# Attention scored a head at a time, and a planner that may move casts and two-tensor operations between engines

## The chip, the cores and the metric

The kernel runs on one core of a Trainium2 chip. The metric is device time in microseconds (us), from several runs of the same program. One execution of it was recorded by the hardware profiler; every row below comes from that one.

## The reference, cut to what matters

A trunk of two layers works on 512 tokens of width 1024. Each layer is a norm, one input projection, three token mixers that read the same normalised input (A windowed attention, B gated DeltaNet, C RWKV-7), an output projection with residual, and a gated MLP with a width-3 convolution.

```python
def banded_window_attention(q, k, v, sink):        # 6 heads, 2 kv heads, 4 query blocks of 128
    s = jnp.einsum('bnqhgd,bnkhd->bnhgqk', qb, kw) * (HEAD_DIM ** -0.5)
    s = jnp.where(valid, s, -jnp.inf)               # +-128 tokens: 2 or 3 key blocks a query block
    m = jnp.maximum(jnp.max(s, -1, keepdims=True), sk)
    p = jnp.exp(s - m)
    p = p / (jnp.sum(p, -1, keepdims=True) + jnp.exp(sk - m))
    o = jnp.einsum('bnhgqk,bnkhd->bnqhgd', p, vw)
...
for l in range(DEPTH):                              # 2
    h = rms_norm(x, norm_mix[l])
    proj = h @ w_in[l]
    mixed = concatenate([attention, deltanet, rwkv](proj))
    x = x + mixed @ w_out[l]
    h = rms_norm(x, norm_ffn[l])
    x = x + conv_ffn(h, ffn_w_up[l], ffn_conv[l], ffn_w_down[l])
return rms_norm(x, norm_final)
```

DeltaNet and RWKV are computed in chunks of 64 tokens, and both need the inverse of many small triangular blocks.

## The kernel before

**Layout and products.** Activations lie as 128 channels by 512 tokens. Every large product is made of pieces of which each operand is split in a high and a low part (type fp32r): activations in `hh`/`hl` (function `split`), weights in `wh`/`wl` (function `weights`). A weight tile comes as `wr` by DMA, 128 x 512 for four blocks of 128 x 128; `wh` is a cast of it (`S.activation(hi, raw, AF.Copy)`, ScalarE, ACT), and `wl` is `wr` minus `wh` (GpSimd, POOL). Function `product` then issues three matmuls a block: `wh` by `hh`, `wh` by `hl`, `wl` by `hh`. There are 408 weight tiles, and three buffers each for `wr`, `wh`, `wl`.

**Stages of a layer**, with times of layer 0: input projections, token shifts (`token_shift`), RWKV preparation (`rwkv_prep`) and the first inversion (`invert`) to about 195 us; the rest of that inversion (`finish_inverse`) and RWKV's scan to about 297; DeltaNet's inversion (`invert_both`) from 297 to 351, and its `finish_inverse` to 373; DeltaNet's scan (`dn_scan`) to 412; gates, output projection (`w_out`) and norm to 468; the MLP's up-projection to 730 and its down-projection to 840. The up-projection goes through 22 pairs a layer of 48 matmuls each: a gate tile (`tr`) and a value tile (`td`). After each pair VectorE (DVE) scales both from PSUM (`TENSOR_TENSOR td<-ps,rb`), makes the convolution's outer taps with four `SCALAR_TENSOR_TENSOR`, multiplies the two and subtracts the high part; ScalarE or VectorE makes the middle taps (`td<-tr,fixed`, `tr<-td,fixed`), and ScalarE the silu and the high part (`p<-tr`).

**invert_both** (lines 837 to 858) is a chain on VectorE of 30 steps: a product into `cv` (`cv<-pair_sq`) and a sum back into `pair_sq` (`pair_sq<-pair_sq,cv`), each step reading what the last wrote. Between, four transposes before and after.

**Attention.** `attn_head` (line 1299) handles one pair of query heads. For each of four query blocks it makes two score matmuls and two fused mask-and-maximum operations on VectorE (`CUSTOM_DVE_ANT_0 cv<-ps,fixed`, maximum in `mx`), then on 128 x 2 numbers the sink's difference (`es`), the negated maximum (`nmx`), the exponential of `es`; two exponentials with sum (`cv<-cv,nmx`, the sum in `den`); `den` plus `es`, its reciprocal; two normalisations (`cv<-cv,den`), transposes on TensorE, a copy to `tr`, and the product with the values. It yields after each block. Three heads a layer; `layer` calls `next(att, None)` five times among the 31 steps of `invert_both` and once after every step of `dn_scan`, and what is left after it.

**What sets the order.** Nothing above is issued as written. `V`, `S`, `G`, `PE` and `SY` are recorders: class `Plan` notes each operation, its reads and writes, and a cost (`price`). `schedule` is a list scheduler over five engines: it places the ready operation with the smallest `prio`, which is minus the longest path of costs behind it minus the number that table `LEAD` gives to the operation's task. 37 names stand in the table, the same number for both layers. It holds an operation back while the tile that it writes has no room, and prices TensorE (PE) at twice the cost after a long idle time (`COLD`) until enough work has been placed (`WARM`). A VectorE operation of two tensors that starts while POOL is busy is priced longer (`contend`). An operation with an alternative (`other`) goes to whichever of two engines is free first: here copies and scalings of float32 may move between ScalarE and VectorE, but none that writes fp32r, and no operation of two tensors. The trace names line 516, where `call` is made, for nearly every instruction; so rows are told apart by operation and tile.

## Time and profile before

| | before |
|---|---|
| three runs, us | 1677.74, 1678.78, 1680.12 |
| the profiled execution, us | 1681.65 |
| its span, us | 1679.5 |
| TensorE busy | 1531.1 us, 91%, 11500 matmuls |
| VectorE | 1083.1 us, 64% |
| ScalarE | 736.2 us, 44% |
| GpSimd | 645.2 us, 38% |
| DMA | 126.07 MB |

The span is the time from the first to the last recorded instruction; about 2 us of the profiled execution lie outside it. A share of busy time is an average over stages. The windows below tell them apart: for each stretch, its length, then busy time and count for PE, PEld (weight loads), DVE, ACT, POOL, then the TensorE clock that was granted as a share of 2.4 GHz.

### The profile page before, as it was taken

What the parts mean: (1) busy time and instruction counts of PE and PEld (TensorE: products, weight loads), DVE (VectorE), ACT (ScalarE), POOL (GpSimd) and SP (SyncE); (2) the same over time, 40 slices, a digit from 0 to 9 for tenths busy, and PEclk for the clock granted to TensorE, in tenths of its full rate; (3) what the DMA queues carried; (4) which work ended last, traced back from release to release, by engine and by line L of the source; (5) the groups of instructions that cost most, each with busy time, mean ns of one, the idle gap of its engine ahead of it and who ended that gap; (6) DMA issues with size and microseconds to landing.
All of it is one profiled execution on the core that took longest, in us unless ns stands there. A gap on an engine that the chain in (4) does not pass through costs nothing. (4 is left out here: it accounts for less than half of the span.)

```text
span 1679.5 us, 29012 instructions
## 1 busy us (share of the span) xinstructions
PE 1531.1 (91%) x11500; PEld 1192.8 (71%) x11500; DVE 1083.1 (64%) x1689; ACT 736.2 (44%) x1399; POOL 645.2 (38%) x510
## 2 busy tenths in 40 slices
PE   7999787589999999999999996966899999999996
PEld 5677665367777777788876775644677877777885
DVE  7799977967437666740058998789654566766101
ACT  5565345454543433332236544355544433334221
POOL 5422332010555554555552232410017454555553
PEclk9999889779999999999999997996799999999998
DMA  6312303010233333333342121120003333333332
GB/s 177 84 34 76 70 20 89 13 34 2 71 91 100 94 89 95 94 106 112 108 105 64 47 75 39 54 86 1 27 14 89 94 88 95 95 93 88 115 91 85
DMA packets 230536, 126.07 MB, mean 75 GB/s; under 512 B 23656, under 2 KB 221416, under 8 KB 230400
## 3 DMA queue, kind: packets, MB, share of 16 engines
q1 hardware_dynamic: 228624, 121.02, 25.8%
q10 hardware_dynamic: 1776, 3.20, 0.7%
q8 instruction: 90, 1.47, 0.3%
q14 instruction: 46, 0.38, 0.1%
HBM read 117.84 MB, written 6.34 MB: 74 GB/s over the span
## 5 line engine op out<-in xcount | busy, mean ns | idle before, releaser
L516 POOL TENSOR_TENSOR wl<-wr,wh 128x512 fp32r<-128x512 f32 (+1 forms) x408 | 558.1, 1379 | 830.1 <-ACT wh L516 667.9
L516 PE MATMUL ps<-hh,wh 128*128 128x512 f32 x1248 | 457.6, 399 | 6.9 <-ACT wh L516 6.9
L516 ACT ACTIVATE wh<-wr 128x512 fp32r<-128x512 f32 (+1 forms) x408 | 243.5, 616 | 495.9 <-PE ps L516 433.9
L516 PE MATMUL ps<-hh,wl 128*128 128x512 f32 x1248 | 452.9, 398 | 7.4 <-POOL wl L516 5.3
L516 PE MATMUL ps<-hl,wh 128*128 128x512 f32 x1248 | 451.6, 394 | 0.0
L516 PEld LDWEIGHTS ps<-hh,wl 128*128 128x128 f32 x1248 | 232.7, 187 | 84.2 <-POOL wl L516 30.3
L516 PEld LDWEIGHTS ps<-hh,wh 128*128 128x128 f32 x1248 | 233.6, 188 | 69.8 <-ACT wh L516 16.2
L516 PEld LDWEIGHTS ps<-hl,wh 128*128 128x128 f32 x1248 | 233.8, 188 | 51.7 <-issue 3.4
L516 DVE TENSOR_TENSOR p<-ps,p 128x512 f32<-128x512 f32 (+2 forms) x72 | 38.2, 551 | 197.4 <-PE ps L516 197.1
L516 PE MATMUL ps<-p,wh 128*128 128x512 f32 x512 | 158.2, 389 | 0.0
L516 DVE TENSOR_TENSOR td<-ps,rb 128x512 f32<-128x512 f32 (+1 forms) x64 | 43.7, 688 | 136.4 <-PE ps L516 136.3
L516 PEld LDWEIGHTS ps<-p,wh 128*128 128x128 f32 x512 | 96.1, 188 | 19.9
L516 DVE SCALAR_TENSOR_TENSOR tr<-td,fixed,tr 128x511 f32<-128x511 f32 x88 | 105.3, 1197 | 0.6 <-ACT tr L516 0.4
L516 PE MATMUL ps<-p,wl 128*128 128x512 f32 x256 | 99.8, 390 | 0.0
L516 ACT ACTIVATE p<-p 32x256 f32<-32x256 f32 (+3 forms) x112 | 66.0, 589 | 16.1 <-DVE p L516 11.2
L516 PE MATMUL ps<-fixed,cv 128*128 128x128 f32 x168 | 36.6, 338 | 38.8 <-ACT cv L516 35.7
L516 DVE SCALAR_TENSOR_TENSOR td<-tr,fixed,td 128x511 f32<-128x511 f32 x88 | 70.8, 805 | 0.3
L516 PE MATMUL ps<-p,p 32*32 32x32 f32 (+2 forms) x1232 | 56.1, 253 | 14.9 <-DVE p L516 11.3
L516 DVE TENSOR_TENSOR tr<-tr,td 128x512 f32<-128x512 f32 x44 | 67.3, 1529 | 1.6
L516 ACT ACTIVATE p<-ps 64x256 f32<-64x256 f32 (+4 forms) x113 | 44.9, 401 | 52.7 <-PE ps L516 33.3
L516 PEld LDWEIGHTS ps<-sm,p 64*64 64x64 f32 x1344 | 49.4, 145 | 24.6 <-DVE sm L516 12.9
L516 PEld LDWEIGHTS ps<-p,p 32*32 32x32 f32 (+1 forms) x1232 | 51.3, 143 | 21.5 <-DVE p L516 12.1
(170 smaller groups left out, 2089.5 us busy)
## 6 DMA issues: line engine op xcount, KB each, us to landing
wr<-ffn_w_up SPq DMA_DIRECT2D x176, 256.0 KB, 2.8
wr<-w_in SPq DMA_DIRECT2D x88, 256.0 KB, 2.8
wr<-ffn_w_down SPq DMA_DIRECT2D x80, 256.0 KB, 2.9
p<-scr ACTq DMA_DIRECT2D x12, 256.0 KB, 5.1
wr<-w_in SPq DMA_DIRECT2D x24, 128.0 KB, 2.6
wr<-w_out SPq DMA_DIRECT2D x32, 96.0 KB, 2.6
wr<-w_out SPq DMA_DIRECT2D x16, 192.0 KB, 2.6
p<-xt SPq DMA_DIRECT2D x8, 256.0 KB, 4.5
```

The costliest lines, as they stand in the source:

```text
L516: tc.keep_in_program_order(call(*args, **kw))
```

## The change

Four things are changed.

1. `attn_head` handles a head as a whole. All eight score matmuls and mask-and-maximum operations come first and keep their scores in eight `cv` tiles; `es`, `nmx` and the exponential of `es` are made once on 128 x 8 numbers, then come eight exponentials, one `den` plus `es`, one reciprocal, and after these the four blocks' normalisations, transposes and products. It yields seven times a head, each phase a group of its own for `LEAD`.
2. `other` gives more operations an alternative: casts that write fp32r (`wh`, `hh`, the high parts `p`, `cv`, `at` of the MLP's gates) may go to VectorE, and a `tensor_tensor` of SBUF tiles with 128 or more columns may move between VectorE and GpSimd.
3. `LEAD` has a number for each task of each layer (letters `a` and `b`), each phase of `attn_head` and each `token_shift`, some 120 in all.
4. `schedule` prices TensorE's clock by equal stretches (`BEAT`) of the planned time: one with too little weighted work in it (`DOWN`, `WEIGHT`) makes matmuls cost twice later on, until one with enough (`UP`) has passed. An operation that was GpSimd's and goes to VectorE is now priced longer beside a busy GpSimd too. `wake` looks again at what blocks a held operation. `hh` and `hl` ask for one buffer instead of two, which `tile` overrides as before (64).

```diff
 LEAD = {
-    "attn_head0": -17500, "attn_head1": 13500, "attn_head2": 4300, "attn_proj": 281000, "dn_gates": 100400, "dn_out0": 5100,
...
+    "attn_head0a.0": -125700, "attn_head0a.1": 35000, "attn_head0a.3": -50200, "attn_head0a.4": 1596100, "attn_head0a.5": 341900, "attn_head0a.6": -258200,
...
     def other(self, o, name, reads, writes):
-        if not self.flexible or not writes or len(reads) < 1 or "float32r" in str(writes[0].dtype) or reads[0].dtype != F32:
+        if not writes or not reads:
             return None
...
-        if o.eng == "DVE" and name == "tensor_copy":
+        if o.eng == "DVE" and name == "tensor_copy" and src.dtype == F32:
...
+        if name == "tensor_tensor" and not psum and n >= 128 and len(dst.shape) == 2 and o.eng in ("DVE", "POOL"):
+            e, f, cost = ("POOL", self.nc.gpsimd, 180 + 2.3 * n) if o.eng == "DVE" else ("DVE", self.nc.vector, 165 + 1.04 * n)
+            return e, f.tensor_tensor, o.args, o.kw, cost
...
-                if t - free[e] > self.COLD:
-                    cold, heat = True, 0.0
-                if cold:
+                while t >= edge:
+                    slow = here < (self.UP if slow else self.DOWN) * self.BEAT
+                    here, then, edge = then, 0.0, edge + self.BEAT
+                if slow:
                     cost *= 2
...
-            elif o.contend and e == "DVE" and free["POOL"] > t:
+            elif e == "DVE" and (o.contend or o.eng == "POOL") and free["POOL"] > t:
                 cost += min(cost, free["POOL"] - t)
...
     def attn_head(l, tq, q, k, vt, dst):
-        po = ps("r")
-        for nb in range(4):
...
+        scs = [[cv() for g in range(2)] for nb in range(4)]
+        mxt, nmx, es, den = (tiny(8, tag=tag) for tag in ("mx", "nmx", "es", "den"))
+        for nb, (k0, k1) in enumerate(span):
...
+                PE.matmul(pss[:, :W], q[hs, P * nb : P * nb + P], k[hs, P * k0 : P * k0 + W], start=True, stop=True)
+                V.tensor_tensor_reduce(scs[nb][g][:, :W], ...
+        yield
+        V.tensor_tensor(by(es), sinkb[l][:, tq : 6 : 3].unsqueeze(1).broadcast_to([P, 4, 2]), by(mxt), sub)
+        V.tensor_scalar(nmx, mxt, -1.0, None, mult)
+        S.activation(es, es, AF.Exp)
+        for nb, (k0, k1) in enumerate(span):
...
+                S.activation(scs[nb][g][:, :W], scs[nb][g][:, :W], AF.Exp, bias=nmx[:, u], accum_out=den[:, u])
+        yield
+        V.tensor_tensor(den, den, es, add)
+        V.reciprocal(den, den)
+        po = ps("r")
+        for nb, (k0, k1) in enumerate(span):
...
+                V.tensor_scalar(scs[nb][g][:, :W], scs[nb][g][:, :W], den[:, u], None, mult)
...
```

How instructions stand now is told by both orders. First, VectorE inside `invert_both` of layer 0: `pair_sq` and `cv_563` are the chain's tiles, `mx`, `es` and `den` attention's. Before, one query block's operations lie between the steps at a time:

```order
L516 TENSOR_TENSOR pair_sq<-pair_sq,cv_563 128x2x14x17
L516 TENSOR_TENSOR cv_563<-pair_sq 128x468
L516 ISA cv_589,mx_591<-ps_592,fixed 128x384
L516 ISA mx_591 128x1
L516 TENSOR_TENSOR pair_sq<-pair_sq,cv_563 128x2x13x18
L516 TENSOR_TENSOR cv_563<-pair_sq 128x456
L516 ISA cv_590,mx_591<-ps_593,fixed 128x384
L516 ISA mx_591 128x1
L516 TENSOR_TENSOR es_595<-fixed,mx_591 128x2
L516 TENSOR_TENSOR pair_sq<-pair_sq,cv_563 128x2x12x19
```

Now, in the same chain:

```order
L546 CAST wh_816<-wr_815 128x512
L546 TENSOR_TENSOR cv_563<-pair_sq 128x260
L546 TENSOR_TENSOR pair_sq<-pair_sq,cv_563 128x2x26x5
L546 TENSOR_TENSOR cv_563<-pair_sq 128x300
L546 TENSOR_TENSOR pair_sq<-pair_sq,cv_563 128x2x25x6
L546 TENSOR_TENSOR den_575<-den_575,es_574 128x8
L546 RECIPROCAL den_575<-den_575 128x8
L546 TENSOR_TENSOR cv_563<-pair_sq 128x336
L546 TENSOR_SCALAR cv_569<-cv_569,den_575 128x384
L546 TENSOR_SCALAR cv_571<-cv_571,den_575 128x256
L546 TENSOR_SCALAR cv_565<-cv_565,den_575 128x256
L546 TENSOR_SCALAR cv_567<-cv_567,den_575 128x384
```

The whole head's `den` stands near the chain's start, four normalisations and a weight cast stand on VectorE between its steps, and after them the chain runs long stretches without a row of attention.

Second, VectorE in the up-projection of layer 0, the work of one pair. Before:

```order
L516 TENSOR_TENSOR td_1142<-ps_1135,rb_848 128x512
L516 TENSOR_TENSOR tr_1132<-ps_1125,rb_848 128x512
L516 TENSOR_SCALAR td_1133<-tr_1132,fixed 128x512
L516 SCALAR_TENSOR_TENSOR tr_1143<-td_1142,fixed,tr_1143 128x511
L516 SCALAR_TENSOR_TENSOR td_1133<-tr_1132,fixed,td_1133 128x511
L516 SCALAR_TENSOR_TENSOR tr_1143<-td_1142,fixed,tr_1143 128x511
L516 SCALAR_TENSOR_TENSOR td_1133<-tr_1132,fixed,td_1133 128x511
L516 TENSOR_TENSOR tr_1124<-tr_1124,td_1133 128x512
L516 TENSOR_TENSOR p_1134<-tr_1124,p_1134 128x512
```

Now:

```order
L546 CAST wh_1113<-wr_1112 128x512
L546 CAST wh_1120<-wr_1119 128x512
L546 TENSOR_TENSOR td_1106<-ps_1099,rb_812 128x512
L546 TENSOR_SCALAR tr_1107<-td_1106,fixed 128x512
L546 SCALAR_TENSOR_TENSOR tr_1107<-td_1106,fixed,tr_1107 128x511 x2
L546 CAST wh_1129<-wr_1128 128x512
L546 TENSOR_TENSOR tr_1096<-ps_1089,rb_812 128x512
L546 TENSOR_SCALAR td_1097<-tr_1096,fixed 128x512
L546 SCALAR_TENSOR_TENSOR td_1097<-tr_1096,fixed,td_1097 128x511 x2
L546 TENSOR_TENSOR tr_1088<-tr_1088,td_1097 128x512
L546 CAST p_1098<-tr_1088 128x512
L546 TENSOR_TENSOR p_1098<-tr_1088,p_1098 128x512
```

In this pair three weight casts and the cast of the gate's high part have come to VectorE, some of them ahead of or between the four taps.

Third, TensorE at the end of `dn_scan` of layer 0: `ps<-p,sm` is the scan, `ps<-hh,wh` and its like are the output projection, `ps<-td,fixed` a sum of `dn_out`. Before:

```order
L516 MATMUL ps_795<-p_541,sm_776 64x64 x2
L516 MATMUL ps_815<-p_541,sm_797 64x64 x2
L516 MATMUL ps_818<-p_541,sm_817 64x64 x2
L516 MATMUL ps_850<-hh_832,wl_853 128x512
L516 MATMUL ps_861<-hh_832,wl_864 128x512
L516 MATMUL ps_820<-td_819,fixed 128x512
L516 MATMUL ps_850<-hh_834,wh_852 128x512
```

Now (`at` holds queries, keys and values, `tr` the transposed probabilities):

```order
L546 MATMUL ps_745<-p_541,sm_744 64x64 x2
L546 MATMUL ps_764<-at_436,at_508 128x256
L546 MATMUL ps_765<-at_436,at_508 128x256
L546 MATMUL ps_784<-td_783,fixed 128x512
L546 MATMUL ps_696<-tr_711,at_456 64x128
L546 MATMUL ps_696<-tr_724,at_456 64x128 x3
L546 MATMUL ps_696<-tr_737,at_456 64x128 x2
L546 MATMUL ps_696<-tr_713,at_456 64x128
L546 MATMUL ps_696<-tr_726,at_456 64x128 x3
L546 MATMUL ps_696<-tr_739,at_456 64x128 x2
L546 MATMUL ps_787<-td_786,fixed 128x512
L546 MATMUL ps_814<-hh_792,wh_816 128x512
```

The last head's scores, the second head's products with the values and, further on, the last head's transposes and products now follow the scan, among the matmuls of the output projection.

Over the whole program TensorE's passes stay at 11500. Of the 408 weight casts, all ScalarE's before, 220 are VectorE's: 88 of 176 in the up-projection, 75 of 96 in the down-projection, 18 of 32 in the output projection, 39 of 104 in the mixers. VectorE also has 40 casts of gate parts. In the mixers 41 operations of two 128 x 512 tensors, net, have gone from VectorE to GpSimd.

## Rows read from the trace of the kernel before

**Rows 1.** Page: busy us, share of the span and instructions of each engine

```profile
PE 1531.1 (91%) x11500; PEld 1192.8 (71%) x11500; DVE 1083.1 (64%) x1689; ACT 736.2 (44%) x1399; POOL 645.2 (38%) x510
```

**Rows 2.** Windows of layer 0: length; PE, PEld, DVE, ACT, POOL; PEclk, DMA, GB/s

```profile
74.00:195.00 121.00, 110.35 (x1010) 87.64 (x1008) 113.29 (x168) 65.58 (x125) 36.40 (x26) 0.99 0.28 70
...
272.00:297.00 25.00, 18.44 (x175) 13.02 (x174) 23.61 (x37) 17.96 (x37) 1.28 (x1) 0.86 0.21 64
297.00:351.00 54.00, 35.12 (x278) 22.21 (x276) 50.87 (x108) 25.87 (x70) 4.12 (x4) 0.75 0.04 11
351.00:373.00 22.00, 18.64 (x349) 15.05 (x351) 11.68 (x32) 10.21 (x25) 2.11 (x2) 0.53 0.21 61
373.00:412.00 39.00, 35.85 (x706) 28.23 (x703) 30.21 (x94) 22.74 (x67) 4.20 (x5) 1.00 0.01 2
412.00:468.00 56.00, 55.38 (x419) 43.65 (x416) 24.77 (x37) 24.05 (x41) 26.54 (x20) 1.00 0.23 66
468.00:730.00 262.00, 257.50 (x1097) 204.99 (x1096) 169.74 (x195) 104.14 (x165) 133.57 (x94) 0.99 0.32 93
```

**Rows 3.** Window of invert_both, only the chain's own tile `pair_sq`: DVE, then POOL

```profile
297.00:351.00 54.00, 42.95 (x66) 0.22 (x1) 0.75 0.04 11
```

**Rows 4.** Waits of PEld in that window: total us, times, longest us

```profile
PEld ps L516 <- ACT cv L516: 19.6, 5, 9.3
```

**Rows 5.** Attention's tiles `den`, `es`: count, ns min/median/max, first and last start

```profile
L516 ACT ACTIVATE cv<-cv,den x38: 492/509/617, 309.8 to 1228.3; 128x256 f32<-128x256 f32 x20, 128x384 f32<-128x384 f32 x18
L516 DVE TENSOR_TENSOR den<-den,es x24: 148/154/163, 309.3 to 1227.9; 128x2 f32<-128x2 f32 x24
L516 DVE RECIPROCAL den<-den x24: 165/166/167, 309.5 to 1228.1; 128x2 f32<-128x2 f32 x24
L516 DVE TENSOR_SCALAR cv<-cv,den x10: 351/410/421, 364.2 to 1228.3; 128x384 f32<-128x384 f32 x6, 128x256 f32<-128x256 f32 x4
...
L516 DVE TENSOR_TENSOR es<-fixed,mx x24: 150/160/486, 307.9 to 1225.7; 128x2 f32<-128x2 f32 x24
```

**Rows 6.** Tiles `td`, `wl`: 512-column operations on DVE and POOL, ns min/median/max

```profile
L516 DVE SCALAR_TENSOR_TENSOR tr<-td,fixed,tr x88: 736/751/1779, 487.7 to 1546.3; 128x511 f32<-128x511 f32 x88
...
L516 DVE TENSOR_SCALAR td<-tr,fixed x40: 489/514/1597, 515.5 to 1554.6; 128x512 f32<-128x512 f32 x40
L516 DVE TENSOR_TENSOR cv<-cv,td x24: 678/692/1806, 121.6 to 1115.1; 128x512 f32<-128x512 f32 x24
...
L516 POOL TENSOR_TENSOR wl<-wr,wh x408: 389/1297/2285, 14.8 to 1654.6; 128x512 fp32r<-128x512 f32 x136
```

**Rows 7.** Groups by form: busy us, mean ns, idle before it

```profile
L516 ACT ACTIVATE wh<-wr 128x512 fp32r<-128x512 f32 x388 | 236.2, 628 | 463.4 <-PE ps L516 401.9 <-issue 35.2 <-DMA wr<-ffn_w_down 7.0
...
L516 POOL TENSOR_TENSOR tr<-tr,tr 128x512 f32<-128x512 f32 x32 | 46.9, 1466 | 18.5 <-ACT tr L516 16.4 <-DVE tr L516 2.0
```

**Rows 8.** Timeline of DVE and POOL, up-projection, then of DVE in invert_both: start, duration

```profile
561.40 1.78 DVE L516 SCALAR_TENSOR_TENSOR tr<-td,fixed,tr 128x511 f32<-128x511 f32 x1
563.10 0.74 DVE L516 SCALAR_TENSOR_TENSOR td<-tr,fixed,td 128x511 f32<-128x511 f32 x1
...
564.50 1.81 POOL L516 TENSOR_TENSOR wl<-wr,wh 128x512 fp32r<-128x512 f32 x1 [1.87 <-ACT wh L516]
569.49 1.29 POOL L516 TENSOR_TENSOR wl<-wr,wh 128x512 fp32r<-128x512 f32 x1 [3.19 <-ACT wh L516]
...
303.18 1.28 DVE L516 TENSOR_TENSOR cv<-pair_sq 128x168 f32<-128x168 f32 x1
304.49 0.33 DVE L516 TENSOR_TENSOR pair_sq<-pair_sq,cv 128x168 f32<-128x168 f32 x1
```

**Rows 9.** Windows of 42 us in the up- and the down-projection, columns as in group 2

```profile
546.00:588.00 42.00, 41.53 (x180) 33.33 (x179) 29.10 (x35) 17.01 (x27) 22.32 (x16) 1.00 0.33 94
756.00:798.00 42.00, 42.00 (x186) 34.66 (x185) 3.60 (x5) 12.36 (x21) 23.28 (x19) 1.00 0.38 110
```

**Rows 10.** Waits of PEld over the whole span: total us, times, longest us

```profile
PEld ps L516 <- POOL wl L516: 30.3, 57, 1.1
```

79 lines of the change are left out of this document (41 added, 38 removed), and 23 rows, old and new, of the table LEAD.

## The prediction

> **What bounds the kernel now.** I read the busy shares first, then the windows by stage, then who waits for whom inside a stage, then durations of single operations. TensorE is busy 91% of the span [rows 1], but that is an average over three kinds of stage. In the MLP and the output projection TensorE is the bound: 257.50 of 262 us in the up-projection, 55.38 of 56 in the stage before it [rows 2]. There only two things help: fewer matmuls, which the change doesn't bring (11500 passes on both sides), or fewer gaps. In the mixers VectorE is the bound or near it: 113.29 of 121 us up to 195 us, 23.61 of 25 us from 272 to 297, 50.87 of 54 us in the window of `invert_both` [rows 2]. In the last of these TensorE runs at 0.75 of its clock and in the next, from 351 to 373, at 0.53, so near its lower level of 1.2 GHz, after having had little to do [rows 2]. In the scan, 39 us, all four engines are under 36 us: a chain that hops between engines sets its length.
>
> Inside `invert_both` one thing must be seen: the chain's own operations take 42.95 us of the 54 [rows 3], and VectorE spends about 8 more on attention and others. TensorE waits 19.6 us there for attention's `cv` [rows 4], which looks like the cost of doing four query blocks one after the other. It is not: nothing behind the window can start until the chain on VectorE has ended, so TensorE would only wait elsewhere.
>
> In the up-projection a second bound shows. In 42 us TensorE passed 180 matmuls, in as long a piece of the down-projection 186 [rows 9]. Six matmuls at 42/186 = 0.226 us are 1.35 us in 42, over 262 us 8.5 us a layer, 17 for both. These are stalls on a late `wl` (30.3 us in 57 waits over the span [rows 10], most of them there). Why it is late: a tap that takes 0.74 us took 1.78 where POOL's subtraction ran too, and a `wl` that takes 1.29 took 1.81 beside the taps [rows 8]. VectorE and POOL there do not run at the same time but one after the other.
>
> **The change part by part.** All sums are in us of the profiled execution: 1681.65, 2.9 above the median of the three runs, 1678.78. I apply the difference to both.
>
> *Attention's small operations.* `es`, `den`+`es` and the reciprocal fall from 24 to 6 each: 18 x (0.160 + 0.154 + 0.166) = 8.6 us less on VectorE for both layers [rows 5]. Normalisations go the other way: 16 of 38 come from ScalarE to VectorE, 16 x 0.410 = +6.6 [rows 5]. In `invert_both` VectorE so loses 13 small operations (2.0 us), and three masked maxima that move out of the window (1.7), and gains four normalisations (1.5) and in layer 0 two weight casts (1.0): −1.2 us net in layer 0, −2.2 in layer 1. The removed waits are priced at nothing, because VectorE's chain covers them; were the chain not last there, the most would be the 19.6 us of [rows 4].
>
> *Operations that go from VectorE to POOL.* 41 net in the mixers, 0.69 each if undisturbed [rows 6]: 28 us off VectorE for both layers; on POOL each costs 1.47 [rows 7], 60 us on an engine that has room (36.40 of 121 us [rows 2]). What they cost back is collisions. For one, the chain's operation at 303.18 took 1.28 us beside POOL, and the longer next one 0.33 without [rows 8]: 0.95. The full price is a whole POOL operation, 1.47; the lowest is nothing, where VectorE's neighbour reads PSUM. I take 0.95 inside the chain, where every operation has two SBUF inputs, and about 0.4 elsewhere, where by the mix of VectorE operations some half of the neighbours read PSUM.
>
> *Casts that come to VectorE.* A cast from 128 x 512 to fp32r on VectorE stands in no row; the nearest is the scaling `td<-tr,fixed`, 0.489 to 1.597 us [rows 6]. The lower end is the undisturbed one and the upper one includes a whole POOL operation. I take 0.49 where there is room and keep the upper end for a rival. On ScalarE the same cast costs 0.628 [rows 7], and ScalarE is never the bound, so what leaves it saves nothing.
>
> Stage by stage, for layer 0 then layer 1; the loads come from pricing each VectorE row of both orders at the undisturbed duration of its form. To the end of the first inversion (about 195 us) VectorE loses 7 or 8 tensor operations (5.2), 10 smaller operations that move behind it and a few copies, and takes 11 or 8 weight casts: net −9 us of some 118. VectorE is 94% busy there, so I give **−8 and −8**. From there to the end of RWKV's scan it gains 8.7 and 7.4 us, the smaller operations among them, and POOL 7 and 11 operations. VectorE has idle time in that stretch; a chain that hops can take half: **+4 and +4**. Up to `invert_both`, where VectorE is busy 23.61 of 25 [rows 2], it loses 8.4 and 5.9 us, and gains 4 and 8 collisions at 0.4: about **−6 and −3**, of which I keep −5 in layer 0 since the chain ahead of it got longer. In `invert_both`: −1.2 and five further POOL operations at 0.95, **+3.5**, in layer 0; −2.2 and one more collision, **−1**, in layer 1. In `dn_scan` VectorE loses 8.8 and 10.5 us (20 small operations, seven tensor operations, copies), TensorE the last head's work; the hop chain of the scan itself stays, so half at most: **−4 and −4**. Behind the scan TensorE has what was taken out of it: some 13 us of work up to the gates' sums where 6 stood. That stage is TensorE's (55.38 of 56 [rows 2]), so nothing hides it: **+6 and +6**, next to the scan's −4. Sum: −3.5 and −6, together about −9.5.
>
> *The up-projection.* 88 weight casts and 30 gate casts come to VectorE. Six weight casts and three high parts in three pairs, 9 x 0.49 = 4.4 us in 3 x 11.4 us: VectorE has that time (169.74 of 262 [rows 2]). The bound that matters is the time in which VectorE and POOL exclude each other. With taps (12 x 0.74), scalings and products on the one side and 12 x 1.2 of `wl` on the other, three pairs hold some 27 of 34 us now; with the casts 31 or 32. It stays under the whole, narrowly, and a `wh` that is cast earlier lets POOL start earlier. The ends are −17 (all stalls gone [rows 9]) and +43 (88 x 0.49, each cast pushing POOL's work back in full). I take **−4**, nearer to the end that the stall of today bounds, as VectorE and POOL still have some 5% left.
>
> A rule speaks against this part of the change. The Trainium skill, "SBUF — State Buffer", section "Who interferes with whom", says that casts, copies and scalings on VectorE can take the port pair shared with GpSimd, that whoever issues first holds it for the whole instruction, and that ScalarE never waits for anyone. The trace of this case agrees for the scaling (0.489 against 1.597 [rows 6]) and for the taps [rows 8]; by the rule a cast moved from ScalarE to VectorE is one more holder, and the sum would be +43 at the worst in place of −4.
>
> *Down-projection and output projection.* 75 and 18 casts to VectorE. TensorE is busy there all the time (42.00 of 42 [rows 9]) and VectorE 3.60, so nothing: zero. If the cover were gone, each cast would cost a late `wl` of at most 1.6.
>
> *The clock price* costs nothing by itself; it can only reorder. Where the clock is low, 351 to 373, `finish_inverse` runs behind a chain of 51 rows of VectorE during which TensorE has less than before. I see no work put there that would keep the clock up: zero, with up to −8 a layer (TensorE's 18.64 us at 0.53 [rows 2] would be some 10 at full clock).
>
> **Forecast: −9.5 − 4 = −13.5**, from 1681.65 to 1668 in a profiled execution, from 1678.78 to **1665** in the median.
>
> **The rivals.** *The port holds (slower).* Each cast on VectorE delays POOL's `wl`, and through it TensorE. Price: up to 88 x 0.49 = 43 us; at half, 21.5: 1678.78 − 9.5 + 21.5 = 1691, at two thirds 1698. It decides once VectorE's and POOL's excluding operations fill a pair's 11.4 us. For it: they are at 93 to 97% by my count, and a tap already grows to 1.78. Against: the casts stand between matmul-paced operations, and VectorE's operations on PSUM let POOL through.
>
> *No change.* The gains of VectorE in the mixers are eaten by 20 to 25 more collisions at up to 0.95 us and by the longer tail: −9.5 + 10 = 0, and the up-projection stays: 1679. For it: the 19.6 us of waits lie behind the chain [rows 3, 4].
>
> *More.* VectorE's savings count in full (−1 in each first stage, −4 in the second, −4 and −6 in the scan, so some −10 for both), and the stretch at half clock is kept warm, −8 a layer: 1665 − 10 − 16 = 1639. For it: the time is VectorE's. Against: no work that would keep the clock up.
>
> *The change doesn't do what it says about the clock.* Gathering attention early in `invert_both` leaves TensorE idle later in it, so more matmuls run at 1.2 GHz: the 35.12 us of TensorE in that window at 0.75 [rows 2] at 0.6 would be 44, still under 54, but `finish_inverse` starts colder and the scan's first 10 us cost double: +5 to +10 a layer, 1679 to 1685.
>
> **How the numbers follow.** Forecast 0.40 (1655 to 1675), more 0.18, no change 0.12, the port 0.25, the colder clock 0.05. About 0.2% (3.4 us) is what a measurement of this kernel can tell from no change. Faster is 0.40 + 0.18 = 0.58, same 0.12, slower 0.30. The range leaves out the last quarter or so of "more" below 1635 and the upper half of the port's price above 1698: some 0.05 and 0.12.
>
> **What would show it.** In the changed trace: right, if the window up to the first inversion is some 8 us shorter, if `invert_both` is as long as before with TensorE idle late in it, if the scan is shorter and the stage behind it longer by about 6, and if a pair of the up-projection takes 11.2 to 11.4 us. Wrong, if a pair takes over 11.6 and waits on `wl` in total far over 30.3 us (the port); if the stretch behind `invert_both` has a granted clock near 1 (more); if chain operations of `pair_sq` grow well over 42.95 us together (collisions). What I have least ground for is the price of a cast beside POOL, and how much of VectorE's saved time the hopping chains pass on.

## The result: 3.7% slower

| | before | changed |
|---|---|---|
| median, us (4 runs each) | 1678.66 | 1741.22 |
| lowest to highest, us | 1677.74 to 1680.12 | 1736.11 to 1745.97 |
| the profiled execution, us | 1681.65 | 1736.11 |
| its span, us | 1679.5 | 1734.3 |

The ratio is 1.0371, with a 95% interval of 1.0341 to 1.0402. The forecast was 1665 with a range of 1635 to 1698. The profiled execution is the lowest of the four, 54.8 us of span longer than that of before.

Where the 54.8 us went is read stage by stage. Each boundary is the first or last record of the operations named, to about 0.5 us (layer 0, then layer 1; us). Layer 0 is taken to end with the first `ps<-at,wl` of its down-projection, 1.4 to 1.9 us ahead of its last matmul:

| stage | before | changed | difference |
|---|---|---|---|
| to the end of the first inversion's chain on VectorE | 197.9; 184.5 | 189.1; 170.7 | −8.8; −13.7 |
| to the end of its finish_inverse | 12.1; 11.8 | 30.7; 34.1 | +18.6; +22.3 |
| to the start of invert_both | 87.5; 87.1 | 82.4; 83.5 | −5.1; −3.6 |
| invert_both | 53.7; 53.9 | 54.7; 57.0 | +1.0; +3.2 |
| to the end of dn_scan | 73.4; 73.8 | 66.1; 63.7 | −7.2; −10.1 |
| to the start of the up-projection | 43.0; 43.2 | 60.9; 62.3 | +18.0; +19.1 |
| up-projection | 262.9; 259.7 | 271.9; 272.2 | +9.0; +12.5 |
| down-projection (layer 1: to the end) | 109.5; 125.6 | 110.8; 124.1 | +1.3; −1.5 |

Three places hold nearly all of it: the up-projections +21.5, the stretch from the end of `invert_both` to the up-projection +19.8, and the stretch up to `invert_both` +9.7, where a gain is more than given back. The windows of the changed kernel by the same stages, layer 0, with the columns of [rows 2]:

```profile
189.00:220.00 31.00, 25.00 (x324) 19.23 (x324) 24.28 (x31) 18.87 (x40) 10.49 (x7) 0.78 0.04 10
...
302.00:357.00 55.00, 26.50 (x193) 18.26 (x193) 52.94 (x94) 16.88 (x43) 12.62 (x11) 0.78 0.16 48
357.00:423.00 66.00, 58.52 (x1280) 47.50 (x1274) 40.12 (x113) 29.39 (x74) 11.50 (x11) 0.82 0.01 3
423.00:484.00 61.00, 57.20 (x287) 43.72 (x284) 39.20 (x57) 20.45 (x47) 31.87 (x23) 1.00 0.22 64
484.00:755.00 271.00, 256.79 (x1098) 201.85 (x1097) 217.87 (x259) 63.13 (x99) 127.86 (x97) 1.00 0.31 89
```

In the up-projection VectorE's busy time went from 169.74 us [rows 2] to 217.87, ScalarE's from 104.14 to 63.13, and TensorE's idle time from some 4 us to 14. The waits of PEld in that window (total us, times, longest) have changed their name:

```profile
PEld ps L546 <- ACT wh L546: 11.0, 7, 2.1
PEld ps L546 <- DVE wh L546: 9.3, 9, 1.3
PEld ps L546 <- POOL wl L546: 6.2, 25, 1.0
```

Before, the same waits (window 468 to 730) were mostly for `wl`:

```profile
PEld ps L516 <- POOL wl L516: 10.7, 19, 0.6
PEld ps L516 <- ACT wh L516: 3.6, 4, 2.4
```

In layer 1 they were 11.4 and 1.1 us. Now `wh` is late, whichever engine casts it. Two timelines of the changed kernel say why; the first is VectorE, then GpSimd:

```profile
563.08 0.43 DVE L546 CAST wh<-wr 128x512 fp32r<-128x512 f32 x1 [0.72 <-PE ps L546]
563.71 1.50 DVE L546 CAST wh<-wr 128x512 fp32r<-128x512 f32 x1 [0.20 <-PE ps L546]
...
563.64 1.29 POOL L546 TENSOR_TENSOR wl<-wr,wh 128x512 fp32r<-128x512 f32 x1 [3.02 <-DVE wh L546]
```

A cast alone takes 0.43; the next one, begun 0.07 us after GpSimd's subtraction, took 1.50, and TensorE's matmul at 565.27 waited for it. The second is ScalarE:

```profile
592.78 0.72 ACT L546 ACTIVATE td<-tr,fixed 128x512 f32<-128x512 f32 x1 [6.20 <-DVE tr L546]
593.44 0.63 ACT L546 ACTIVATE tr<-tr 128x512 f32<-128x512 f32 x1
593.98 0.61 ACT L546 ACTIVATE wh<-wr 128x512 fp32r<-128x512 f32 x1
```

ScalarE idled 6.20 us for VectorE's `tr`, because its next instruction was the scaling of a value tile; the weight cast stood two places behind it. VectorE was late since a subtraction and a cast just before had taken 1.67 and 1.51 us beside GpSimd. The scheme repeats every three pairs, with a stall of about 1.6 us and one of 0.84, so some 2.4 us in 36.

### The profile page after: what moved, and what is told of

It reads as the page before. It is cut to its first block, busy times and chain, and to the rows that moved or that the text cites. A ratio compares the mean times of both kernels' runs of the same rounds, so it can differ in the third digit from the quotient of the medians.

```text
span 1734.3 us, 28897 instructions
## 1 busy us (share of the span) xinstructions
PE 1536.6 (89%) x11500; PEld 1190.6 (69%) x11500; DVE 1259.1 (73%) x1875; ACT 554.7 (32%) x1077; POOL 700.4 (40%) x556
## 5 line engine op out<-in xcount | busy, mean ns | idle before, releaser
L546 PE MATMUL ps<-hh,wh 128*128 128x512 f32 x1248 | 478.6, 403 | 45.5 <-DVE wh L546 20.2
L546 PE MATMUL ps<-hh,wl 128*128 128x512 f32 (+1 forms) x1248 | 462.5, 398 | 5.8 <-POOL wl L546 5.5
L546 DVE CAST wh<-wr 128x512 fp32r<-128x512 f32 (+2 forms) x220 | 144.1, 657 | 252.1 <-PE ps L546 223.6
L546 PEld LDWEIGHTS ps<-hh,wl 128*128 128x128 f32 (+1 forms) x1248 | 234.4, 188 | 77.3 <-POOL wl L546 20.6
L546 ACT ACTIVATE wh<-wr 128x512 fp32r<-128x512 f32 x188 | 116.4, 628 | 510.4 <-PE ps L546 475.9
L546 DVE SCALAR_TENSOR_TENSOR tr<-td,fixed,tr 128x511 f32<-128x511 f32 x88 | 82.4, 939 | 2.0 <-ACT tr L546 0.5
L546 POOL TENSOR_TENSOR p<-p,tr 128x512 f32<-128x512 f32 x16 | 21.7, 1359 | 118.2 <-ACT tr L546 72.7
L546 DVE SCALAR_TENSOR_TENSOR cv<-td,fixed,cv 128x510 f32<-128x510 f32 (+1 forms) x72 | 65.3, 929 | 4.1 <-ACT cv L546 2.6
L546 PE MATMUL ps<-sm,p 64*64 64x64 f32 x1344 | 61.0, 237 | 6.8 <-DVE sm L546 5.9
L546 ACT ACTIVATE tr<-p 128x512 f32<-128x512 f32 x46 | 28.9, 629 | 110.9 <-DVE p L546 102.9
```

The source lines that it names most:

```text
L546: tc.keep_in_program_order(call(*args, **kw))
```

## Experiments

Times are medians; "before" in the same sittings lay between 1681.25 and 1683.13, and each ratio is against the one of its own sitting. Stage times come from one profiled execution each.

### The up-projection

**up_casts_act.** Casts to fp32r have no alternative while the up-projection is recorded (`fixed` is true around its loop):

```diff
-        if not writes or not reads:
+        if not writes or not reads or self.fixed and o.eng == "ACT" and "float32r" in str(writes[0].dtype):
             return None
```

> The changed kernel, but in the up-projection the casts to fp32r (weights and gate parts) stay on ScalarE, as before; all else as changed. The changed kernel's up-projections take 271.9 and 272.2 us where before took 262.9 and 259.7. Theory (the casts on VectorE, in line behind the convolution's taps and locked out by GpSimd, make wh late): both come back to 259 to 263 us and the whole goes from 1741 to about 1720; the PEld waits on wh there fall from 20 us a layer to under 4, those on wl rise from 6 to 10 or more. Rival (the time of that stage comes from what the planner orders otherwise there, not from the casts): it stays above 268 us and the whole above 1735.

Measured 1716.9 (ratio 1.0201, 1.0170 to 1.0231). The up-projections took 260.4 and 260.5 us, as before the change, and no other stage moved by more than 3.2. TensorE's waits on `wh` there fell to 1.5 and 1.0 us, those on `wl` rose to 12.0 and 12.6. So the whole +21.5 goes when these casts stay on ScalarE.

**up_weights_act** and **up_gates_act** bar one kind each, by the name of the written tile (`wh` or not `wh`).

> The changed kernel; in the up-projection the weight casts alone stay on ScalarE, the casts of gate parts may go to VectorE (all 40 are there). With both kinds on ScalarE it took 1716.9, with both free 1741. Theory (a late wh is what TensorE waits for, so it is the 44 weight casts a layer): the up-projections come back to 258 to 263 us, whole 1714 to 1722. Rival (VectorE is simply too full, and either kind frees enough or each costs by its time): 264 to 268 us, whole 1726 to 1733.

> The changed kernel; in the up-projection the casts of gate parts alone stay on ScalarE, weight casts may go to VectorE (52 of 88 a layer are there, 44 before this edit), and 16 subtractions of gate parts go to GpSimd. Theory (the weight casts are the cost): the up-projections stay at 270 us or more, whole 1738 to 1750. Rival (VectorE's total decides): 262 to 267 us, whole 1720 to 1732.

Measured 1718.8 (1.0208, 1.0181 to 1.0235), up-projections 261.0 and 261.1; and 1737.4 (1.0330, 1.0301 to 1.0360), up-projections 270.4 and 270.7. The first says that the gate casts alone cost nothing (261.0 against 260.4 with both kinds on ScalarE). The second is not its mirror image, for its 10 us a layer have another cause. TensorE's waits in its up-projection of layer 0 (window 482 to 752), and GpSimd's timeline before one of them:

```profile
PEld ps L546 <- POOL wl L546: 21.2, 33, 1.8
PEld ps L546 <- DVE wh L546: 3.4, 5, 1.3
...
572.61 1.29 POOL L546 TENSOR_TENSOR p<-tr,p 128x512 fp32r<-128x512 f32 x1 [3.33 <-ACT p L546]
573.86 4.40 POOL L546 TENSOR_TENSOR wl<-wr,wh 128x512 fp32r<-128x512 f32 x3
```

Here it is `wl` that is late, as it stands behind a gate's subtraction that the `tensor_tensor` alternative sent to GpSimd. So the changed kernel's loss needs the weight casts on VectorE, but what they would cost there without the gate casts is not shown.

**b_up_casts_free.** The kernel before, with the ban on fp32r lifted in the up-projection alone.

> The kernel before, with one thing of the change: in the up-projection alone casts to fp32r may go to VectorE; the planner then puts 54 of 176 weight casts and 46 casts of gate parts there or leaves them, the rest is as before. Theory (each such cast costs by the port and by standing in VectorE's line): of the changed kernel's +21.4 us for 88 weight casts about 54/88, so +10 to +15 us over before, 1690; all of it in the two up-projections. Rival (the casts are free and the loss comes from elsewhere in the change): within 3 us of before, 1679.

Measured 1684.5 (1.0008, 0.9994 to 1.0022): no difference that can be told. The planner put 27 of 88 weight casts a layer on VectorE here, 44 in the changed kernel. So the cost is not so much a cast: in this plan 27 cost nothing, in the changed kernel's 44 cost 10 us a layer. The theory, a price in proportion, falls.

The changed kernel has a second way out. **no_tt_move** (below) bars only the moves of two-tensor operations and leaves the casts free, in all stages; the planner then puts 27 or 28 weight casts a layer on VectorE, and the up-projections take 257.6 and 257.0 us. Up- and down-projections of both layers together, which don't depend on where the one ends, take 759.5 us before, 780.4 in the changed kernel, 759.0 in up_casts_act, 761.9 in b_up_casts_free and 760.6 in no_tt_move. So the loss needs both new freedoms at once: either one barred, it is gone. The number of casts alone is not shown to decide, since these plans differ in more (with 27 casts ScalarE also makes 34 or 35 of 42 middle taps, in the changed kernel 22 or 23).

**b_w4** and **a_w4.** Four buffers instead of three for `wh` and `wl` in the up-projection, in the kernel before and in the changed one:

```diff
-            hi = plan.tile(bp, [P, WK, m], F32R, tag="wh", bufs=3, name=nm("wh"))
-            lo = plan.tile(bp, [P, WK, m], F32R, tag="wl", bufs=3, name=nm("wl"))
+            hi = plan.tile(bp, [P, WK, m], F32R, tag="wh4" if plan.fixed else "wh", bufs=4 if plan.fixed else 3, name=nm("wh"))
+            lo = plan.tile(bp, [P, WK, m], F32R, tag="wl4" if plan.fixed else "wl", bufs=4 if plan.fixed else 3, name=nm("wl"))
```

> The kernel before with four buffers instead of three for wh and wl in the up-projection alone. Theory (each pair loses 0.33 to 0.44 us there because a wl that VectorE's taps hold up comes too late for TensorE; a buffer more lets GpSimd be a tile further ahead): PEld's waits on wl in the up-projections fall from 22 us to under 8, whole 1660 to 1672. Rival (GpSimd and VectorE take turns at the port whatever the buffers, or the planner puts the subtraction where it was): within 3 us of before.

> The changed kernel with four buffers instead of three for wh and wl in the up-projection; casts free as in the change (37 and 38 of 88 weight casts a layer on VectorE, 44 before this edit). Theory (a weight cast on VectorE costs because it comes late with no tile in hand: it stands behind taps that GpSimd holds up, and three buffers give no slack): the up-projections fall from 272 us to 252 to 260, PEld's waits on wh there from 20 us a layer to under 6, whole 1705 to 1720. Rival (VectorE and GpSimd together are full, so that slack only delays the stall): above 266 us, whole 1730 or more.

b_w4 measured **1665.8** (0.9892, 0.9871 to 0.9914), faster than both kernels. Window of its up-projection in layer 0, PEld's waits in it, and GpSimd's timeline there:

```profile
466.00:719.00 253.00, 252.19 (x1102) 205.61 (x1101) 167.81 (x199) 88.47 (x151) 126.73 (x97) 1.00 0.34 98
...
PEld ps L517 <- ACT wh L517: 2.8, 8, 1.0
PEld ps L517 <- POOL wl L517: 1.7, 3, 0.7
...
559.91 3.97 POOL L517 TENSOR_TENSOR wl<-wr,wh 128x512 fp32r<-128x512 f32 x3 [3.99 <-ACT wh L517]
```

GpSimd now does three subtractions in a row, two of them before the first tap begins at 562.66; the wait on `wl` fell from 10.7 to 1.7 us, and the two up-projections from 522.6 to 504.9 us. The other stages, which were planned a little differently, gave 2.4 us back: −15.3 of span.

a_w4 measured 1700.8 (1.0106, 1.0081 to 1.0131), some 40 us under the changed kernel and a little under the theory's range. Its up-projections took 254.2 and 256.1 with 37 and 38 weight casts on VectorE, and PEld's waits in the first (window 486 to 738) were:

```profile
PEld ps L547 <- POOL wl L547: 4.7, 5, 1.1
PEld ps L547 <- DVE wh L547: 0.6, 1, 0.6
PEld ps L547 <- ACT wh L547: 0.5, 1, 0.5
```

Its window's row is

```profile
486.00:738.00 252.00, 249.45 (x1092) 204.05 (x1091) 190.59 (x226) 71.43 (x117) 149.65 (x106) 1.00 0.34 97
```

VectorE and GpSimd together are busier for each us than in the changed kernel (340 us in 252, against 346 in 271), and TensorE hardly waits. So at 37 casts the two engines were not full. A weight cast came late, and with three buffers nothing was in hand to cover it. What 44 would do with four buffers was not tried; the planner chose 37.

### Attention

**b_attn_head.** The kernel before with the new `attn_head` alone, at the old numbers.

> The kernel before with the new attn_head alone (its phases keep the old LEAD number of their head). Theory (handling a head at a time makes attention late: the last head's products fall behind the scan and push the output projection's matmuls out of it, as in the changed kernel, where the stretch from the end of invert_both to the up-projection grew by 10.7 and 9.1 us): +5 to +9 us a layer, 1689 to 1697. Rival (attn_head is neutral or gains by the fewer small operations, and the tail is LEAD's work): 1673 to 1681.

Measured 1738.8 (1.0339, 1.0321 to 1.0356): by itself as much as nearly the whole loss, and far more than either theory gave. Its windows of `invert_both` and of what follows to the scan's end, then the second of these in the kernel before:

```profile
299.00:351.00 52.00, 16.93 (x175) 12.80 (x175) 48.82 (x92) 17.68 (x46) 2.74 (x3) 0.65 0.05 16
351.00:442.00 91.00, 76.85 (x1290) 60.00 (x1284) 45.26 (x122) 28.14 (x76) 5.73 (x6) 0.77 0.01 2
...
351.00:424.00 73.00, 65.96 (x1277) 52.81 (x1277) 46.17 (x138) 33.89 (x95) 6.31 (x7) 0.86 0.07 20
```

TensorE has 175 matmuls under the chain where it had 278 [rows 2], and the stretch to the scan's end is 91 us long instead of 73, at a lower clock (0.77 for 0.86). Over both layers that stretch costs 38 us and the one behind the scan 20; in the changed kernel only the second is longer. Of attention's 228 matmuls a layer (records), before had 95 under `invert_both`, 130 up to the scan's end and none behind; b_attn_head 49, 98 and 60; the changed kernel 62, 74 and 84. The order tells where this comes from. `layer` calls `next(att)` five times in `invert_both`'s loop and eight in the scan's. That was enough for the old form's 12 yields a layer. The new form yields six times a head, not seven as the account of the change has it: after the maxima, after the exponentials and after each block, 18 times a layer. So 13 calls leave five steps, the last head's exponentials and four blocks, to be recorded after the scan (the texts below count 21 phases and eight left, since they take the copy at a head's end as one). These five hold 60 matmul records, just the 60 that stand behind the scan. The planner gives out PSUM and SBUF tiles in the order of recording, and so holds back what is recorded late. Whether larger numbers in `LEAD` could bring it forward was not run.

**b_attn_calls42** and **b_attn_calls** change only these calls, in b_attn_head's kernel: 7 and 16 of them, or 10 and 16.

```diff
-            if i % 6 == 5:
+            if i % 4 == 3:
                 next(att, None)
...
-            next(att, None)
+            for _ in range(2):
+                next(att, None)
```

> The kernel before with the new attn_head and calls to next(att) so counted (7 among the steps of invert_both, 16 after those of the scan) that by the order 61 of attention's 144 matmuls stand ahead of the end of invert_both, 83 in the scan, none behind it, as in the kernel before. Theory (where attention's matmuls stand is what the new form cost, and the form itself costs nothing): 1676 to 1686. Rival (with ten calls 1704.9: the form itself, a head's maxima at once on VectorE and its products at once on TensorE, lengthens invert_both and the scan wherever the calls put it): 1695 to 1710.

> The kernel before with the new attn_head, as in the run that took 1738.8, and the larger number of calls to next(att) (10 among the steps of invert_both, 16 after those of the scan). Theory (the new form of attention loses only because the calls were left as they were): the 28.2 and 30.1 us from the end of invert_both to the up-projection go, whole 1670 to 1688. Rival (batches of a head are bad in themselves: eight masked maxima on VectorE before the first product, under a chain on VectorE): 1710 or more.

b_attn_calls42 measured 1693.5 (1.0058, 1.0036 to 1.0081), b_attn_calls 1704.9 (1.0138, 1.0118 to 1.0157). So in this kernel some 45 of the 56 us were the calls. In b_attn_calls42 every stage is within 2 us of before, but `invert_both`, which is 6.6 and 6.4 longer:

```profile
295.50:355.70 60.20, 34.14 (x225) 23.45 (x225) 57.95 (x125) 27.23 (x74) 5.61 (x5) 0.71 0.08 22
```

VectorE holds there 15 masked maxima instead of 10 (+2.7 us) and eight normalisations (+3.1), which before stood on ScalarE, 11 copies of 32 x 256 instead of 4 (+2.0), and 1.4 us less of `es`, `den` and reciprocals; the chain's own products took 1.9 us more. On an engine whose chain ends last each of them counts in full. Neither theory holds as stated: the form is not free, and its price is VectorE's, not TensorE's.

**calls** and **up_act_calls22** make the same edit in the changed kernel (ten calls and two a step; fifteen and two a step, with the casts barred).

> The changed kernel with one edit: layer calls next(att) ten times among the steps of invert_both instead of five, and twice after every step of the scan instead of once, so that the 21 phases that the new attn_head yields are all recorded before the scan ends (5 + 8 calls were enough for the old 12 phases, and leave 8 phases recorded behind the scan now). By the order none of attention's matmuls stands behind the scan then (54 and 57 of 144 in the changed kernel). Theory (the planner gives PSUM and SBUF tiles in the order of recording, so what is recorded late runs late; that made the tail): the stretch from the scan's end to the up-projection falls from 60.9 and 62.3 us to 43 to 50, whole from 1741 to 1710 to 1725. Rival (the tail is LEAD's, or the work only moves into the chain on VectorE and lengthens invert_both as much): whole 1735 or more.

> The changed kernel with the up-projection's casts to fp32r on ScalarE and next(att) called fifteen times among the steps of invert_both and twice after every step of the scan, so that by the order 124 and 116 of attention's 144 matmuls stand ahead of the end of invert_both's chain. Theory (TensorE is idle in that window and attention's matmuls cost nothing there): 1685 to 1700, the two gains of 24 us (casts) and 15 to 25 us (tail) added. Rival (attention's masked maxima, 0.48 to 0.61 us each, lengthen the chain on VectorE by what they save): invert_both 8 us longer a layer, whole 1705 to 1717.

calls (`i % 3 == 2`, and two calls a step of the scan) measured 1771.3 (1.0533, 1.0508 to 1.0558): none of attention's matmuls stands behind the scan any more, and the tail (the stretch from the scan's end to the up-projection) shrank from 60.9 and 62.3 to 47.4, as the theory had it, and 55.1, which is above its 43 to 50. So 13.5 of the tail's 18.0 us of growth and 7.2 of its 19.1 went with attention's matmuls. But two gate projections fell behind `invert_both` in layer 0 and the scan grew by 26.7 there, in layer 1 the stretch up to `invert_both` grew by 16; the whole time missed the theory's range. up_act_calls22 measured 1723.0 (1.0250, 1.0220 to 1.0280): tail 42.3 and 45.2, but `invert_both` 62.1 in layer 0, and the scan 12.6 longer than in the changed kernel; the whole missed both ranges. That the new numbers of `LEAD` fit only the order that they were found with is my reading; no run shows it.

**old_attn.** The changed kernel with the old attention and its old numbers.

> The changed kernel with the old attn_head (a query block at a time) and its old LEAD numbers; all else as changed. Theory (handling a head at a time takes attention's matmuls out of the window of invert_both and puts them behind the scan: 62 of 228 in that window and 84 behind the scan where before had 95 and none): the stretch from the end of invert_both to the up-projection, 127.0 and 126.0 us in the changed kernel, falls to 116 to 119, none of attention's matmuls stand behind the scan, whole about 1720. Rival (the tail is made by the new LEAD of the scan and the outputs, whatever attention's form): above 124 us in both layers, whole above 1735.

Measured 1792.3 (1.0664, 1.0640 to 1.0689), the slowest of all, with the tail at 51.2 in both layers, but the scan at 102.4 and 88.5: all three gate projections of layer 0 had moved behind `invert_both`. By its letter the rival came true, but with the gate projections there the run can't tell the two apart. It does show that the tail is not attention's alone: only some dozen of attention's matmuls stand behind the scan here, all within 2.3 us of its end, and the tail is still 8 us longer than before. 190 matmuls of the output projection stand in it, 191 in the changed kernel, 173 before.

### The stretch up to invert_both

Four kernels: **prep_lead_old** has the old numbers for the tasks of these stages; **no_tt_move** and **casts_act** edit `other` in the changed kernel; **b_tt_move** is the kernel before with the lines of the `tensor_tensor` alternative and its price added.

```diff
no_tt_move
-        if name == "tensor_tensor" and not psum and n >= 128
+        if False and name == "tensor_tensor" and not psum and n >= 128
casts_act
-        if not writes or not reads:
+        if not writes or not reads or o.eng == "ACT" and "float32r" in str(writes[0].dtype):
prep_lead_old, among others
-    "attn_proj0a": -64200, "finish_inverse0a": -269200,
+    "attn_proj0a": 281000, "finish_inverse0a": -58500,
```

> The changed kernel with the old LEAD numbers for every task up to RWKV's scan and DeltaNet's preparation (projections, token shifts, RWKV preparation and scan, invert, attention's projections, the first finish_inverse); the casts, the moves to GpSimd and attn_head stay as changed. The changed kernel needs 30.7 and 34.2 us from the end of the first inversion's chain to the end of its finish_inverse, before 12.1 and 11.8. Theory (TensorE's queue has attention's projection matmuls ahead of finish_inverse, put there by LEAD, and they wait for PSUM that VectorE frees only after the chain): these stretches fall to 12 to 18 us, the start of invert_both comes 10 to 20 us earlier in each layer, whole about 1705 to 1720. Rival (the stretch is long because VectorE collides with the operations moved to GpSimd): still over 25 us, whole above 1735.

> The changed kernel without the alternative for two-tensor operations: none of them moves between VectorE and GpSimd. Theory (what VectorE saves before the first inversion's chain ends is real, 8.8 and 13.7 us there, and is the moves' work): the time to the end of that chain grows by 6 to 10 us a layer, and invert_both loses its added collisions, 2 to 4 us a layer; whole 1741 to 1755. Rival (that gain is only work of TensorE put off behind the chain, where finish_inverse pays for it; the moves bring collisions and no gain): start of invert_both not later than in the changed kernel, whole 1725 to 1738.

> The changed kernel with all casts to fp32r on ScalarE, in every stage. Without those of the up-projection alone it took 1716.9. Theory (VectorE is the bound of the mixers, so 39 weight casts there, at 0.43 us alone and up to 1.5 beside GpSimd, cost 10 to 20 us, and 18 in the output projection some 2 to 4): 1695 to 1707, the gain in the stretches up to invert_both and in the output projection. Rival (in the mixers and the output projection the casts are hidden): 1714 to 1720.

> The kernel before with one thing of the change: two-tensor operations of SBUF tiles may move between VectorE and GpSimd (63 go to GpSimd, 28 come from it), with the wider price for collisions; old LEAD, old attn_head, casts as before. Theory (VectorE is near its limit in the mixers and each move takes 0.69 us from it for about 0.4 us of collisions): 1660 to 1674. Rival (collisions take back all): 1676 to 1690.

| us to the start of invert_both, layer 0; layer 1 from the last matmul of layer 0 | to the chain's end | finish_inverse | rest | sum |
|---|---|---|---|---|
| before | 197.9; 184.5 | 12.1; 11.8 | 87.5; 87.1 | 297.5; 283.4 |
| changed | 189.1; 170.7 | 30.7; 34.1 | 82.4; 83.5 | 302.2; 288.3 |
| prep_lead_old (1752.8, ratio 1.0422) | 198.9; 192.2 | 20.9; 17.1 | 83.4; 88.9 | 303.2; 298.2 |
| no_tt_move (1735.9, 1.0327) | 186.7; 177.3 | 35.7; 28.4 | 85.0; 88.7 | 307.4; 294.4 |
| casts_act (1728.0, 1.0275) | 188.3; 174.8 | 29.2; 40.3 | 86.0; 85.0 | 303.5; 300.1 |
| b_tt_move (1716.1, 1.0211) | 198.6; 187.2 | 20.6; 15.3 | 85.2; 86.7 | 304.4; 289.2 |

With the old numbers the long `finish_inverse` shrinks by 10 and 17 us, and the stage ahead of it grows by 10 and 21. So VectorE's earlier end is paid for by work put off, and it comes with the new numbers and not with the moves to GpSimd: no_tt_move has the earlier end without them, b_tt_move and prep_lead_old have the moves without it. In the changed kernel, 185 to 195 us, windows of 5 us and TensorE's one large wait there:

```profile
185.00:190.00 5.00, 0.00 (x0) 0.00 (x0) 4.86 (x6) 0.84 (x3) 0.00 (x0) 0.92 0.00 0
190.00:195.00 5.00, 4.05 (x10) 3.21 (x11) 5.00 (x7) 4.86 (x10) 1.46 (x1) 0.50 0.00 0
...
PE ps L546 <- DVE td L546: 7.0, 1, 7.0
```

TensorE stands still for 7.0 us, because its next matmul, of attention's value projection, needs a PSUM bank that VectorE drains only behind the inversion's last transposes; then 48 matmuls of the value and one query projection run until 205.6, the first at half clock, ahead of most of `finish_inverse`. Before, these matmuls ran during the chain (24 matmuls from 185 to 190 us). Barring the moves to GpSimd, or the casts, makes the sum worse by 5 to 6 and 1 to 12 us: under the new numbers they help here. The whole times of casts_act and b_tt_move lie outside both of their ranges, and prep_lead_old's outside its theory's; b_tt_move loses most in the scan, 84.5 and 84.2 us for 73.4 and 73.8. What costs the last 5 us a layer I could not single out.

### The clock price

**b_clock** is the kernel before with the new loop over `BEAT` in `schedule`, **a_old_clock** the changed kernel with the old one:

```diff
a_old_clock
-                while t >= edge:
-                    slow = here < (self.UP if slow else self.DOWN) * self.BEAT
...
-                if slow:
+                if t - free[e] > self.COLD:
+                    cold, heat = True, 0.0
+                if cold:
                     cost *= 2
```

> The kernel before with the change's price of TensorE's clock alone (stretches instead of an idle time); old LEAD, attn_head and alternatives. Theory (this price moves little): 1675 to 1686. Rival (it is what costs the 5 us a layer up to invert_both that no other part has explained, by putting attention's projections behind the first inversion to keep TensorE busy): the stretch from the chain's end to the end of the first finish_inverse grows by more than 5 us over 12.1 and 11.8, whole 1688 or more.

> The changed kernel with the old price of TensorE's clock (an idle time); new LEAD, attn_head and alternatives. By the order little moves: attention's projections still stand ahead of the first finish_inverse. Theory (LEAD, not the clock's price, sets that order, so the 30.7 and 34.1 us from the end of the first inversion's chain to the end of its finish_inverse stay): within 8 us of the changed kernel, 1733 to 1749. Rival (the new price costs here as it does with the old LEAD, 37 us there): 1700 to 1725.

b_clock measured 1718.0 (1.0216, 1.0198 to 1.0235): the rival's 1688 or more, though only 4 us of it a layer lie in `finish_inverse`; the scan grew by 7.2 and 6.6. a_old_clock measured 1772.6 (1.0539, 1.0515 to 1.0563): `finish_inverse` stays at 30.6 and 35.0, as the theory says, but the scan is 80.3 and 76.4 us long, so both whole times are missed. With the old numbers the new price costs 37 us, with the new ones it saves some 30. The mean granted clock over the span of the profiled execution is 0.946 before, 0.947 in the changed kernel (0.940 to 0.947 over its four runs), 0.934 in b_clock and 0.935 in a_old_clock: the pair of new price and new numbers holds the clock, and does not raise it.

## Why the prediction was wrong

**VectorE's saving in the first stage** came out near its number (−8 a layer; −8.8, −13.7), but that was luck. I took it from the operations that leave VectorE, above all the moves to GpSimd. In layer 0 the chain ends as early without the moves (no_tt_move, 186.7), in layer 1 about half of the gain is left (177.3), and with the moves and the old numbers there is none (prep_lead_old, 198.9 and 192.2). **"+4 and +4" behind it** is the first step that failed: it measured +18.6 and +22.3, then −5.1 and −3.6. I counted VectorE's load in that stretch and not what stands ahead of `finish_inverse` on TensorE, though the order showed it: 48 matmuls of attention's value and query projections, behind a wait of 7.0 us.

**invert_both** (+3.5 and −1; +1.0 and +3.2) was nearly right in the sum, not in its parts. The chain's own operations there took 45.66 us where [rows 3] has 42.95:

```profile
302.00:357.00 55.00, 45.66 (x66) 0.23 (x1) 0.78 0.16 48
```

That is 2.7 us for layer 0, where I had priced five collisions at 0.95 each, 4.75; the rest of VectorE's work there, priced at −1.2, came out at −1.1. In layer 1 the growth has another cause, which I had at nothing: VectorE, which waited 1.1 us in that window before, waits 4.0 us there now, 2.2 for scores from TensorE and 1.8 for ScalarE.

**The scan −4 and the tail +6** is the second step: −7.2 and −10.1, and +18.0 and +19.1. The mechanism was named, its size was a third. I took 13 us of TensorE's work; the window between the scan's end and the up-projection has 287 matmuls in the changed kernel (above), and in the kernel before

```profile
424.00:468.00 44.00, 43.91 (x187) 34.12 (x186) 20.50 (x26) 23.10 (x39) 26.54 (x20) 1.00 0.29 83
```

that is 100 more, 84 of attention and the rest the output projection's, which the scan used to take in. TensorE is busy 13.3 us longer there (57.20 for 43.91), where I had set 13 for 6, and idle 3.7 us more. And I took the third place of the order as something that a priority had chosen; b_attn_head, b_attn_calls42 and calls show that the unchanged calls to `next(att)` put attention's matmuls there. What made the rest of the tail, 4.4 and 11.9 us, is open.

**The up-projection, −4** is the third, and the largest: +21.5. The rival with the port had that price, 21.5 at its half, and a chance of 0.25. But its reason was not the one, so its price came true by luck: it had `wl` late and the two engines full, and its sign, waits on `wl` far over 30.3 us, did not come (26.2 over the span). a_w4 shows that VectorE and GpSimd have room, and the waits that `wh` is late. I asked whether the engines had time, not whether the operation that TensorE waits for would be on time in its line. The rule of the Trainium skill that I weighed ("SBUF — State Buffer", "Who interferes with whom") agrees with the trace: a cast went from 0.43 to 1.50 us beside GpSimd. ScalarE, which by the rule never waits for the port, was late with a cast all the same, since the cast stood in line behind an operation that idled 6.20 us for VectorE's result.

**"More"** did not come: the clock is no higher (0.946 and 0.947 in the mean). **"The down-projection: zero"** held (+1.3, −1.5).

What stays open: 5 us a layer up to `invert_both`, a part of the tail, and why the numbers of one part of `LEAD` move so much elsewhere.

## What to carry to other kernels

Before work is moved to an engine with time to spare, ask which instruction the bound engine waits for next, what stands ahead of that one in the new queue, and how many buffers lie between; one more buffer was worth 1.1% here, and no move alone gained anything. When a task is cut in more steps, look at the code that steps through it: calls that were enough for 12 left 5 of 18 behind the stage that was to hide them. A table of priorities fitted to one set of rules is not a neutral ground: under the old table the casts freed in the up-projection alone made no difference that can be told, and attention's new form, the two-tensor moves and the clock's price cost 35 to 57 us each, so a part is judged by stages, not by the whole time.

## What the runs showed of the hardware

The cast from 128 x 512 f32 to fp32r on VectorE has no row before; its durations in the changed kernel (ns min/median/max) are

```profile
L546 DVE CAST wh<-wr x220: 196/427/2684, 28.8 to 1709.7; 128x512 fp32r<-128x512 f32 x100, 128x256 fp32r<-128x256 f32 x8, 128x96 fp32r<-128x96 f32 x2
```

so 0.43 us alone, under the 0.49 taken from the scaling [rows 6]. By form, and beside them the casts that stayed on ScalarE in the same execution:

```profile
L546 DVE CAST wh<-wr 128x512 fp32r<-128x512 f32 x200 | 135.7, 680 | 230.2 <-PE ps L546 201.8 <-issue 13.6 <-DMA wr<-ffn_w_down 12.5
L546 ACT ACTIVATE wh<-wr x188: 612/632/637, 15.2 to 1705.6; 128x512 fp32r<-128x512 f32 x188
```

In the mean the 512-column cast takes 0.680 us on VectorE, more than ScalarE's 0.628 [rows 7]. Which cast is slow is a matter of what had begun first. Of the 200, 127 began while no operation of GpSimd ran, and every one of them took 0.43. Of the 73 that began during one, 58 took longer, 0.48 to 1.56 us and one 2.68. On ScalarE 112 of the 188 ran beside GpSimd, and all took 0.61 to 0.64. For a cast that another engine waits for, ScalarE was the steadier place here.
